# Copies that form the weight sums wait for a tile of the gated projection or of the attention

## The chip, the cores and the metric

The kernel runs on one core of a Trainium2 chip. The core has TensorE (PE) for matmuls, with its weight loads shown apart (PEld), VectorE (DVE), ScalarE (ACT), GpSimd (POOL) and SyncE (SP). DMAs are commands in the queue of the engine that issues them, here nearly all SP or POOL; the bytes are moved by 16 DMA engines that all queues share. The metric is the device time of the program in microseconds (us): 1652.23 as the median of three runs, 1650.91 to 1655.87.

## The reference

One layer of a decoder on 1024 tokens of width 1024, in float32. From a normalised input one projection makes queries, six key and value blocks, gates, a pooling input and merge-gate logits:

```
h = rms_norm(x, norm_mix);  proj = h @ w_in
a = nsa_attention(q, kv, gates, ...) @ w_branch_attn    # compressed, selected and window branch
b = pool_mixer(u_pool, pool_w, pool_scale) @ w_branch_pool
ga, gb = split(sigmoid(g_merge), 2)
x = x + (ga * a + gb * b) @ w_out
h = rms_norm(x, norm_mlp)
x = x + square(relu(h @ w_ff1)) @ w_ff2;  return rms_norm(x, norm_final)
```

There are 8 heads of 64 in two groups, blocks of 64 keys, a window of 512, and an MLP of width 4096.

## The kernel before

Every float32 operand is split into a high part, which ScalarE rounds to the matmul's format (hi, L179), and a low part, the rest, which POOL or VectorE subtracts (lo, L82). A product is three matmuls: high by high (L77), high by low (L78, L79). Weights come through one helper, `load`: a raw tile of 128x512 (`wraw`, 4 buffers, a DMA on SP, L178), then `whi` and `wlo` (3 buffers each).

The stages, in the order of the program:

1. First key/value block (L230 to 268), to 53 us: x and weights are loaded and multiplied into eight PSUM banks.
2. Second key/value block and compression (L283 to 381): `block2` in eight token tiles, `compress` for keys and values; `keys` rotates and transposes keys.
3. Query blocks (`qblock`, L383 to 400), twice eight token tiles: 24 matmuls of 256 columns, `q` made by ScalarE (L392, two buffers), rotated by POOL (L145 to 149), stored to DRAM as `qd` (L395).
4. Pooling mixer (`pool_in`, `pool_mix`, four groups): 48 matmuls of 512 columns for each group, then 6 more. The low parts of the weights are made by POOL.
5. Gated projection (L480 to 501): eight blocks m of 48 matmuls for the gate and 24 for the branch, each giving two tiles `gb` (two buffers, stored to DRAM as `gbd`). Low parts by POOL, three per block.
6. Attention: 32 pairs (query tile i, head pair hp), scores and softmax of one pair woven with transposes and values of the pair before. Between them `ga_terms` is fed in, a gate projection of eight weight blocks, two low parts each, by POOL. A finished pair writes its part of `oT` (L666).
7. Merge: the attention's output projection, `ta` and `gb` loaded back (L796, L797, `gb` with one buffer), then `w_out`.
8. The MLP. It uses seven block products in place of eight, for which sums of weight blocks are needed.

These sums are the change's subject. Each of 32 is a tile of 1 MB in DRAM: a plain copy of one block from DRAM to DRAM on SP's queue (L208), then a DMA on POOL's queue that adds a second block, or an earlier sum, to it (L213, L216). The function `weight_sums` is a generator: one step issues one copy and the accumulation of the step before.

```
206                         d = dram.tile([P, 2048], F32, name=f"ws{layer}{fh}{p}{h}")
208                         nc.sync.dma_start(d, a[layer][fh, m0, k0, h])
213                             nc.gpsimd.dma_start(d_, src, accum_op=ADD, max_dma_last_dim=2048)
```

The program calls `next(sums)` once in each block m of the gated projection (L481) and then from `advance` (L689) as the attention goes on. That doesn't set when a copy runs. The framework orders each engine's instructions when the program is built, by its own estimate of when each could start, and waits are semaphores that it places for tiles read and written. The copies read an input and write a fresh tile, so nothing holds them back, and in the order that it finds they stand on SP from the second key/value block on, between the loads and stores of that stage, with the accumulations on POOL.

Of the kernel before, what the change touches and what calls it, by code (L numbers as in the profile page):

```python
# [17 lines left out]
P = 128  # L18
S = 1024
# [30 lines left out]
def build(tc, a, out, dbg=None):  # L50
    nc = tc.nc
# [141 lines left out]
    tad = [[dram.tile([P, HALF], F32, name=f"tad{m}_{h}") for h in range(2)] for m in range(NK)]  # L193


    wsum = {}

    def weight_sums():
        late = []
        for layer in ("w_ff1", "w_ff2"):  # L200
            for fh in range(2):
                for p in (7, 6, 5, 3):
                    for h in range(2):
                        d = dram.tile([P, 2048], F32, name=f"ws{layer}{fh}{p}{h}")
                        wsum[layer, fh, p, h] = d
                        (m0, k0), (m1, k1) = {7: ((0, 0), (1, 0)), 6: ((1, 1), (0, 0)), 5: ((1, 0), (1, 1)),
                                              3: ((0, 1), (0, 0))}[p]
                        nc.sync.dma_start(d, a[layer][fh, m0, k0, h])  # L208
                        prior = {6: 7, 3: 6}.get(p)
                        late.append((d, a[layer][fh, m1, k1, h] if prior is None else wsum[layer, fh, prior, h]))  # L210
                        if len(late) > 1:
                            d_, src = late.pop(0)
                            nc.gpsimd.dma_start(d_, src, accum_op=ADD, max_dma_last_dim=2048)  # L213
                        yield
        for d_, src in late:
            nc.gpsimd.dma_start(d_, src, accum_op=ADD, max_dma_last_dim=2048)  # L216

    sums = weight_sums()


# [201 lines left out]
    with ExitStack() as st:  # L422
# [6 lines left out]
        with ExitStack() as st2:  # L429
# [48 lines left out]
                    pool_mix(*prev)  # L478
                prev = cur
            for m in range(NK):  # L480
                next(sums)  # L481
                gh, gl = load(cols(a["w_in"], C_GB + m * P, P))
                bh, bl = load(cols(a["w_branch_pool"], m * P, P, 0, 4))
                zz = []
                for hf in range(2):
                    sl = slice(hf * HALF, (hf + 1) * HALF)
                    ps = psF.tile([P, HALF], F32, name="psF")
                    mm3(ps, [(gh[:, k], gl[:, k], XH[k][:, sl], XL[k][:, sl]) for k in range(NK)])
                    z = wg.tile([P, HALF], F32, name="z", bufs=3)
                    nc.vector.tensor_tensor(z, ps, rB[:, sl], op=MUL)  # L490
                    nc.scalar.activation(z, z, AF.Tanh, scale=0.5)
                    zz.append(z)
                if m == 0:
                    pool_mix(*prev)
                for hf in range(2):
                    sl = slice(hf * HALF, (hf + 1) * HALF)
                    ps = psF.tile([P, HALF], F32, name="psF")
                    mm3(ps, [(bh[:, k], bl[:, k], mxh[:, k, sl], mxl[:, k, sl]) for k in range(4)])
                    gb = wg.tile([P, HALF], F32, name="gb", bufs=2)
                    nc.vector.scalar_tensor_tensor(gb, zz[hf], 1.0, ps, op0=ADD, op1=MUL)  # L500
                    nc.sync.dma_start(gbd[m][hf], gb)


    octx = ExitStack()
# [2 lines left out]
    with ExitStack() as st:  # L507
# [175 lines left out]
        done, given, summed = 0.0, 0, 0  # L683

        def advance(w):
            nonlocal done, given, summed
            done += w
            while summed < 26 * done / total:
                next(sums, None)  # L689
                summed += 1  # L690
            while given < nterm and given < nterm * done / total:
                next(fill, None)
                given += 1
# [5 lines left out]
        for n in range(len(pairs) + 1):  # L699
            aseq = []  # L700
            if n < len(pairs):
                i, hp = pairs[n]
                if n == 12:
                    sctx.close()
                    psS = pool(sctx, "psS2", bufs=2, space=PSUM)
                u, aseq = units_a(i, hp, q)
                if hp % 2:
                    def nxt(j=2 * i + hp // 2 + 1):
                        nonlocal q, qnext
                        if j < 2 * NT:  # L710
                            q = split_q(qnext)
                            if j + 1 < 2 * NT:
                                qnext = load_q((j + 1) // 2, (j + 1) % 2)
                    aseq.append(nxt)
            na, nslot = len(aseq), max(1, sum(o for _, o in bseq))
            ia = k = 0
            for fn, slot in bseq or [(None, True)]:
                if fn is not None:
                    fn()
                if slot:  # L720
                    k += 1
                    while ia < na and ia * nslot < k * na:
                        aseq[ia]()
                        ia += 1
                    advance(bw / nslot)
            assert ia == na
            if n < len(pairs):
                bseq, bw = units_b(u), weight[n]
        for _ in fill:
            pass  # L730
        for _ in sums:
            pass
        sctx.close()
        dump("oT", oT)
    psTctx.close()
# [289 lines left out]
```

## Time and profile before

| | |
|---|---|
| median of three runs | 1652.23 us (1650.91 to 1655.87) |
| profiled execution: time, span | 1656.69 us, 1654.9 us |
| granted TensorE clock, mean | 0.943 |
| busy share of the span | PE 89%, PEld 74%, DVE 61%, ACT 46%, POOL 10% |
| DMA queues, share of 16 engines' span | q1 (SP) 32.8%, q0 (POOL) 11.5% |
| HBM read, written | 186.52 MB, 83.89 MB |
| copies of the weight sums on SP | 32 issued, 33.3 to 319.1 us |
| accumulations on POOL | 32 issued, 41.4 to 341.4 us |

The span runs from the first to the last instruction. The stages stand in it so: first key/value block to 53 us, second block with compression to about 150, query blocks to 265, pooling mixer to 356, gated projection to 490, attention to 850, merge to about 1000, MLP to the end. A granted clock of 1.00 is 2.4 GHz, 0.50 is 1.2. A DMA share is the mean busy share of 16 engines and can come out above 1 where packets overlap. "Landing" is the time from a DMA's issue to its last byte.

### The profile page before, as it was taken

How to read it: one execution, taken by the hardware profiler on the slowest of the kernel's cores; microseconds unless marked ns; L12 is line 12 of the kernel's file. 1: busy time of each engine (PE TensorE's matmuls, PEld its weight loads, DVE VectorE, ACT ScalarE, POOL GpSimd, SP SyncE). 2: the span in 40 equal slices, each digit the busy share in tenths (PEclk: the TensorE clock that was granted, in tenths of full speed). 3: DMA queues.
4: the chain of work that ended last, by engine and by line, in shares of the span. 5: the costliest groups of instructions: out<-in, count | busy, mean ns of one | idle time of the engine just before them, and what ended most of it. 6: DMA issues, size and time to landing. Idle time of an engine off the chain costs nothing.

```text
span 1654.9 us, 20716 instructions
## 1 busy us (share of the span) xinstructions
PE 1480.2 (89%) x7369; PEld 1222.5 (74%) x7369; DVE 1001.7 (61%) x1928; ACT 758.6 (46%) x1561; POOL 169.1 (10%) x206
## 2 busy tenths in 40 slices
PE   8766554669999999999998989999999999999995
PEld 6755453558877788887876878888888888888874
DVE  5554101331118888887765575766789656669984
ACT  4332110121227877777753344557434453764441
POOL 2111333122220000000001010000000000001020
PEclk9878677789999999999999999999999999999997
DMA  8999999962231110010046533333333333333322
GB/s 304 289 286 222 262 275 280 230 144 83 77 102 46 38 46 21 33 33 26 27 136 214 148 104 107 94 100 97 97 95 97 96 96 96 96 96 97 96 63 102
DMA packets 130137, 204.67 MB, mean 124 GB/s; under 512 B 9840, under 2 KB 62832, under 8 KB 129520
## 3 DMA queue, kind: packets, MB, share of 16 engines
q1 hardware_dynamic: 112992, 169.78, 32.8%
q0 software_dynamic: 16896, 33.56, 11.5%
q8 instruction: 58, 0.95, 0.2%
q14 instruction: 47, 0.39, 0.1%
q10 hardware_dynamic: 144, 0.00, 0.0%
HBM read 186.52 MB, written 83.89 MB: 163 GB/s over the span
## 4 chain that ended last, share of the span: by engine, by line
PE 71%; DMA 3%; DVE 3%; ACT 2%; issue 1%; POOL 0%; POOLq 0%; DVEq 0%; SPq 0%; ACTq 0%
PE psm L79 14%; PE psm L77 14%; PE psm L78 14%; PE oacc L659 5%; PE psT L648 4%; PE psF L79 3%; PE psF L78 3%; PE psF L77 3%; DMA gb<-gbd 3%; PE psS L553 2%; PE psS L554 2%; PE psG L77 2%; PE psG L78 2%; PE psG L79 2%; PE psS L556 1%
## 5 line engine op out<-in xcount | busy, mean ns | idle before, releaser
L78 PE MATMUL psm<-mv,whi 128*128 128x512 f32 x896 | 351.9, 393 | 0.0
L77 PE MATMUL psm<-mv,whi 128*128 128x512 f32 x896 | 351.8, 393 | 0.0
L79 PE MATMUL psm<-mv,wlo 128*128 128x512 f32 x896 | 351.7, 393 | 0.0
L82 DVE TENSOR_TENSOR wlo<-wraw,whi 128x512 fp32r<-128x512 f32 x288 | 197.9, 691 | 109.9 <-ACT whi L858 70.3
L858 ACT CAST whi<-wraw 128x512 fp32r<-128x512 f32 x224 | 138.8, 620 | 247.9 <-PE psm L78 185.9
L78 PEld LDWEIGHTS psm<-mv,whi 128*128 128x128 f32 x896 | 169.0, 189 | 37.0
L77 PEld LDWEIGHTS psm<-mv,whi 128*128 128x128 f32 x896 | 168.9, 189 | 36.9
L79 PEld LDWEIGHTS psm<-mv,wlo 128*128 128x128 f32 x896 | 168.9, 188 | 36.8
L179 ACT CAST whi<-wraw 128x512 fp32r<-128x512 f32 x112 | 69.4, 622 | 175.3 <-PE psF L78 77.0
L79 PE MATMUL psF<-xh,wlo 128*128 128x512 f32 x192 | 79.1, 412 | 50.7 <-POOL wlo L82 50.7
L652 DVE TENSOR_TENSOR pl<-psT,ph 128x512 fp32r<-128x512 f32 (+1 forms) x160 | 101.9, 646 | 31.1 <-ACT ph L651 29.7
L754 POOL TENSOR_TENSOR sqa<-sqa,sq 128x512 f32<-128x512 f32 x24 | 33.1, 1381 | 803.0 <-ACT sq L750 803.0
L651 ACT CAST ph<-psT 128x512 fp32r<-128x512 f32 (+1 forms) x160 | 87.6, 555 | 50.1 <-PE psT L648 48.4
L563 DVE TENSOR_REDUCE nm<-psS 128x1 f32<-128x64 f32 (+8 forms) x192 | 99.6, 539 | 16.4 <-PE psS L556 9.0
L82 POOL TENSOR_TENSOR wlo<-wraw,whi 128x512 fp32r<-128x512 f32 x48 | 64.3, 1350 | 422.5 <-ACT whi L179 299.3
L77 PE MATMUL psF<-bhi,xh 128*128 128x256 f32 (+1 forms) x192 | 63.9, 335 | 40.0 <-ACT q L392 15.1
L79 PEld LDWEIGHTS psF<-xh,wlo 128*128 128x128 f32 x192 | 38.3, 199 | 60.2 <-POOL wlo L82 52.0
L77 PE MATMUL psF<-xh,whi 128*128 128x512 f32 x192 | 78.4, 408 | 2.8 <-ACT q L392 2.8
L78 PE MATMUL psF<-xl,whi 128*128 128x512 f32 x192 | 78.0, 406 | 0.0
L77 PEld LDWEIGHTS psF<-bhi,xh 128*128 128x128 f32 x192 | 43.9, 230 | 42.8 <-ACT q L392 15.4
L564 ACT ACTIVATE pS<-psS,nm 128x64 f32<-128x64 f32 (+8 forms) x128 | 67.9, 532 | 8.3 <-DVE nm L563 7.9
L838 ACT CAST mv<-mt 128x512 fp32r<-128x512 f32 x96 | 59.1, 617 | 20.0 <-DVE mt L836 15.5
(241 smaller groups left out, 3119.1 us busy)
## 6 DMA issues: line engine op xcount, KB each, us to landing
wraw<-wsw_ff SPq DMA_DIRECT2D x128, 256.0 KB, 3.1
wraw<-in_w_ff SPq DMA_DIRECT2D x96, 256.0 KB, 3.1
wsw_ff<-in_w_ff POOLq DMA_DIRECT2D x16, 1024.0 KB, 27.2
wsw_ff<-wsw_ff POOLq DMA_DIRECT2D x16, 1024.0 KB, 18.0
wraw<-in_w_in SPq DMA_DIRECT2D x40, 256.0 KB, 2.9
wraw<-in_w_out SPq DMA_DIRECT2D x32, 256.0 KB, 3.1
xt<-in_x SPq DMA_DIRECT2D x8, 512.0 KB, 5.2
qd<-q SPq DMA_DIRECT2D x16, 256.0 KB, 8.7
```

Source lines behind the costliest of these rows:

```text
L77: nc.tensor.matmul(ps, lhsT=sh, rhs=mh, start=first and i == 0, stop=False, skip_group_check=more)
L78: nc.tensor.matmul(ps, lhsT=sh, rhs=ml, start=False, stop=False, skip_group_check=more)
L79: nc.tensor.matmul(ps, lhsT=sl, rhs=mh, start=False, stop=last and i == n - 1, skip_group_check=more)
L82: eng.tensor_tensor(lo, src, f(hi), op=SUB)
L179: nc.scalar.copy(h, v)
L563: nc.vector.tensor_reduce(nm, v, axis=AX.X if flat else AX.XY, op=MAX, negate=True)
L564: nc.scalar.activation(p if flat else p.rearrange("p (a n) -> p a n", a=2), v, AF.Exp, bias=nm, accum_out=sm)
L648: nc.tensor.transpose(ps[:, j, e], src[e][:, c0:c0 + P], ident)
L651: nc.scalar.copy(ph[:, :n], ps[:, :n])
L652: nc.vector.tensor_tensor(pl[:, :n], ps[:, :n], f(ph[:, :n]), op=SUB)
L659: nc.tensor.matmul(o, lhsT=v, rhs=part[:rows, j], start=gi == 0 and j == 0 and part is ph, stop=2 * gi + j == nb - 1 and part is pl)
L858: nc.scalar.copy(hi, raw)
```

## The change

A copy of a weight sum now goes to POOL's queue. Ahead of it, on SP, four words (16 bytes) of a tile just computed are stored into the sum's own tile. The copy writes over them, so it must wait for that store, and the store for the tile. The tiles are kept in a list `made`: in the gated projection the last `gb` of the block before (L505 after the change; the first block has none, so seven sums start there), in the attention the part of `oT` of the pair before last, one sum at most per pair, 25 in all, the last of them behind the last part of `oT`.

```diff
--- before.py
+++ after.py
@@ -193,7 +193,8 @@
     tad = [[dram.tile([P, HALF], F32, name=f"tad{m}_{h}") for h in range(2)] for m in range(NK)]
 
 
-    wsum = {}
+
+    wsum, made = {}, []
 
     def weight_sums():
         late = []
@@ -205,7 +206,8 @@
                         wsum[layer, fh, p, h] = d
                         (m0, k0), (m1, k1) = {7: ((0, 0), (1, 0)), 6: ((1, 1), (0, 0)), 5: ((1, 0), (1, 1)),
                                               3: ((0, 1), (0, 0))}[p]
-                        nc.sync.dma_start(d, a[layer][fh, m0, k0, h])
+                        nc.sync.dma_start(d[0:1, 0:4], made.pop())
+                        nc.gpsimd.dma_start(d, a[layer][fh, m0, k0, h])
                         prior = {6: 7, 3: 6}.get(p)
                         late.append((d, a[layer][fh, m1, k1, h] if prior is None else wsum[layer, fh, prior, h]))
                         if len(late) > 1:
@@ -478,7 +480,8 @@
                     pool_mix(*prev)
                 prev = cur
             for m in range(NK):
-                next(sums)
+                if made:
+                    next(sums)
                 gh, gl = load(cols(a["w_in"], C_GB + m * P, P))
                 bh, bl = load(cols(a["w_branch_pool"], m * P, P, 0, 4))
                 zz = []
@@ -499,6 +502,7 @@
                     gb = wg.tile([P, HALF], F32, name="gb", bufs=2)
                     nc.vector.scalar_tensor_tensor(gb, zz[hf], 1.0, ps, op0=ADD, op1=MUL)
                     nc.sync.dma_start(gbd[m][hf], gb)
+                made[:] = [gb[0:1, 0:4]]
 
 
     octx = ExitStack()
@@ -683,11 +687,8 @@
         done, given, summed = 0.0, 0, 0
 
         def advance(w):
-            nonlocal done, given, summed
+            nonlocal done, given
             done += w
-            while summed < 26 * done / total:
-                next(sums, None)
-                summed += 1
             while given < nterm and given < nterm * done / total:
                 next(fill, None)
                 given += 1
@@ -724,12 +725,19 @@
                         ia += 1
                     advance(bw / nslot)
             assert ia == na
+            if n >= 2 and summed < 25 * done / total:
+                i, hp = pairs[n - 2]
+                made[:] = [oT[0:1, hp, i * P:i * P + 4]]
+                next(sums, None)
+                summed += 1
             if n < len(pairs):
                 bseq, bw = units_b(u), weight[n]
         for _ in fill:
             pass
-        for _ in sums:
-            pass
+        while len(wsum) < 32:
+            made[:] = [oT[0:1, 3, S - 4:S]]
+            next(sums)
+        next(sums, None)
         sctx.close()
         dump("oT", oT)
     psTctx.close()
```

What it moves on the engines is seen in their order. On SP in the second query block and at the start of the pooling mixer, before the change (`qd` are stores of queries, `wsw_ff` the sums, `s` the mixer's weights):

```order
L208 DMA wsw_ff_5786<-in_w_ff 16x16384
L395 DMA qd_104<-q 128x512
L395 DMA qd_105<-q 128x512
L208 DMA wsw_ff_5961<-in_w_ff 16x16384
L208 DMA wsw_ff_6122<-in_w_ff 16x16384
L395 DMA qd_106<-q 128x512
L395 DMA qd_107<-q 128x512
L208 DMA wsw_ff_6270<-in_w_ff 16x16384
L208 DMA wsw_ff_6437<-in_w_ff 16x16384
L395 DMA qd_108<-q 128x512
L395 DMA qd_109<-q 128x512
L208 DMA wsw_ff_6610<-in_w_ff 16x16384
```

The same place after it:

```order
L397 DMA qd_102<-q 128x512
L178 DMA wraw<-in_w_in 128x4x128 x2
L397 DMA qd_103<-q 128x512
L397 DMA qd_104<-q 128x512
L397 DMA qd_105<-q 128x512
L397 DMA qd_106<-q 128x512
L397 DMA qd_107<-q 128x512
L397 DMA qd_108<-q 128x512
L397 DMA qd_109<-q 128x512
L435 DMA s<-in_pool_w 128x4x128
L178 DMA wraw<-in_w_in 128x4x128 x3
```

Six copies stood among these stores and loads; none does now. On POOL in the pooling mixer before the change (`pwl` and `wlo` are low parts, `u` a tile's margin):

```order
L213 DMA wsw_ff_6610<-in_w_ff 512x512
L82 TENSOR_TENSOR pwl<-s,pwh 128x512
L82 TENSOR_TENSOR wlo<-wraw,whi 128x512 x2
L213 DMA wsw_ff_6766<-wsw_ff_6437 512x512
L213 DMA wsw_ff_6918<-wsw_ff_6610 512x512
L439 MEMSET u 128x16
L82 TENSOR_TENSOR wlo<-wraw,whi 128x512
L213 DMA wsw_ff_7089<-in_w_ff 512x512
L82 TENSOR_TENSOR wlo<-wraw,whi 128x512
L213 DMA wsw_ff_7235<-in_w_ff 512x512
L213 DMA wsw_ff_7387<-wsw_ff_6766 512x512
L439 MEMSET u 128x16
```

After it, to the first sum in the gated projection:

```order
L82 TENSOR_TENSOR pwl<-s,pwh 128x512
L82 TENSOR_TENSOR wlo<-wraw,whi 128x512 x2
L441 MEMSET u 128x16
L82 TENSOR_TENSOR wlo<-wraw,whi 128x512 x2
L441 MEMSET u 128x16
L82 TENSOR_TENSOR wlo<-wraw,whi 128x512 x7
L210 DMA wsw_ff_2524<-in_w_ff 16x16384
L82 TENSOR_TENSOR wlo<-wraw,whi 128x512
L215 DMA wsw_ff_2524<-in_w_ff 512x512
L82 TENSOR_TENSOR wlo<-wraw,whi 128x512 x2
L210 DMA wsw_ff_2633<-in_w_ff 16x16384
```

The accumulations that stood between the mixer's low parts are gone, and the first copy stands behind all of the mixer's low parts and those of the first two blocks of the gated projection. On POOL at the passage from the gated projection to the attention after the change, where before there was only a run of 41 low parts:

```order
L82 TENSOR_TENSOR wlo<-wraw,whi 128x512 x2
L210 DMA wsw_ff_3183<-in_w_ff 16x16384
L82 TENSOR_TENSOR wlo<-wraw,whi 128x512
L215 DMA wsw_ff_3183<-wsw_ff_2743 512x512
L82 TENSOR_TENSOR wlo<-wraw,whi 128x512 x2
L210 DMA wsw_ff_3553<-in_w_ff 16x16384
L215 DMA wsw_ff_3553<-wsw_ff_2853 512x512
L210 DMA wsw_ff_3722<-in_w_ff 16x16384
L82 TENSOR_TENSOR wlo<-wraw,whi 128x512
L215 DMA wsw_ff_3722<-in_w_ff 512x512
L82 TENSOR_TENSOR wlo<-wraw,whi 128x512
L210 DMA wsw_ff_4026<-in_w_ff 16x16384
```

In a block of the gated projection a copy stands ahead of the next block's first low part and the accumulation behind it; in the attention one or two low parts, or none, stand between a copy and the next. On SP at the end of the attention after the change (`tad` stores the gates, `ta` and `gb` are the merge's first loads):

```order
L538 DMA tad_1_139<-z 128x512
L178 DMA wraw<-in_w_branch_attn 128x4x128
L209 DMA wsw_ff_7821<-oT 1x4
L538 DMA tad_0_140<-z 128x512
L209 DMA wsw_ff_7942<-oT 1x4
L178 DMA wraw<-in_w_branch_attn 128x4x128 x2
L538 DMA tad_1_141<-z 128x512
L209 DMA wsw_ff_7946<-oT 1x4
L804 DMA ta<-tad_0_126 128x512
L805 DMA gb<-gbd_0_110 128x512
```

The last two small stores stand close ahead of the merge's first loads, and the last one waits for the end of the attention. On PE, DVE and ACT the same instructions stand before and after; in the second key/value block, the compression and the query blocks some stand a few places earlier or later, and from the gated projection on none does.

## Rows read from the trace of the kernel before

**Rows 1.** Busy time by stretches: stretch, us, busy by engine, clock, DMA share, GB/s
```profile
53.00:150.00 97.00, 63.04 (x389) 58.08 (x387) 54.24 (x163) 34.03 (x87) 10.85 (x13) 0.81 1.07 288
150.00:265.00 115.00, 70.19 (x415) 64.68 (x414) 14.52 (x67) 20.59 (x46) 42.92 (x97) 0.77 1.04 256
265.00:356.00 91.00, 42.18 (x150) 33.44 (x151) 28.02 (x32) 11.41 (x17) 21.23 (x22) 0.70 1.02 233
356.00:490.00 134.00, 132.80 (x584) 109.11 (x583) 28.75 (x41) 27.87 (x44) 30.68 (x25) 1.00 0.27 77
490.00:850.00 360.00, 351.89 (x2286) 286.25 (x2284) 287.48 (x676) 269.83 (x686) 17.51 (x14) 1.00 0.12 36
```

**Rows 2.** DMA view, 60 to 340 us: queues; issues with median landing
```profile
q0 software_dynamic: 15354, 30.50, 61.8%
q1 hardware_dynamic: 14150, 43.13, 43.6%
...
wsw_ff<-in_w_ff POOLq DMA_DIRECT2D x14, 1024.0 KB, 29.2
qd<-q SPq DMA_DIRECT2D x16, 256.0 KB, 8.7
...
wsw_ff<-in_w_ff SPq DMA_DIRECT2D x28, 14.2
```

**Rows 3.** The same of 380 to 480 us, in the gated projection
```profile
q1 hardware_dynamic: 11232, 7.87, 27.1%
...
gbd<-gb SPq DMA_DIRECT2D x12, 256.0 KB, 2.0
```

**Rows 4.** Waits, 53 to 150 us: who waited for whom, total, times, longest
```profile
ACT bhi L179 <- DMA wraw<-in_w_in: 13.5, 7, 5.2
PEld psH L77 <- ACT whi L179: 13.0, 3, 9.6
ACT whi L179 <- DMA wraw<-in_cmp_k_w: 12.8, 2, 11.2
...
ACT whi L179 <- DMA wraw<-in_cmp_v_w: 10.9, 6, 3.5
```

**Rows 5.** Waits, 150 to 265 us
```profile
ACT q L392 <- DMA qd<-q: 66.8, 13, 15.7
```

**Rows 6.** Waits, 265 to 357 us
```profile
PE psF L79 <- POOL wlo L82: 50.7, 3, 23.8
POOL wsw_ff L213 <- DMA wsw_ff<-in_w_ff: 46.0, 6, 12.3
```

**Rows 7.** TensorE in order of time: start, us, instruction, idle before
```profile
80.04 0.28 PE L79 MATMUL psH<-whi,Xl 128*128 128x256 f32 x1
80.16 0.28 PE L77 MATMUL psH<-whi,Xh 128*128 128x256 f32 x1
...
94.29 0.58 PE L77 MATMUL psH<-whi,Xh 128*128 128x256 f32 x1 [9.40 <-ACT whi L179]
...
97.22 0.42 PE L79 MATMUL psH<-whi,Xl 128*128 128x256 f32 x1
97.43 0.42 PE L77 MATMUL psH<-whi,Xh 128*128 128x256 f32 x1
```

**Rows 8.** POOL in order of time, one block of the gated projection
```profile
383.27 1.29 POOL L82 TENSOR_TENSOR wlo<-wraw,whi 128x512 fp32r<-128x512 f32 x1 [6.87 <-ACT whi L179]
386.00 1.29 POOL L82 TENSOR_TENSOR wlo<-wraw,whi 128x512 fp32r<-128x512 f32 x1 [1.43 <-ACT whi L179]
391.43 1.29 POOL L82 TENSOR_TENSOR wlo<-wraw,whi 128x512 fp32r<-128x512 f32 x1 [4.14 <-ACT whi L179]
399.59 1.29 POOL L82 TENSOR_TENSOR wlo<-wraw,whi 128x512 fp32r<-128x512 f32 x1 [6.87 <-ACT whi L179]
```

**Rows 9.** Groups of POOL, 265 to 357 us: count, busy, mean ns, idle before
```profile
L213 POOL DMA_DIRECT2D wsw_ff<-wsw_ff x4 | 4.1, 1015 | 36.1 <-DMA wsw_ff<-in_w_ff 36.1
```

**Rows 10.** Chain of waits after the attention, in order of time
```profile
858.21 6.26 DMA gb<-gbd
```

## The prediction

> **What bounds the kernel now.** I read the busy time by stretches first, since the page's shares are means over stages with different limits. From 356 us on TensorE is the bound: busy 132.8 of 134 us in the gated projection and 351.9 of 360 in the attention, at a granted clock of 1.00, with the DMA engines at 0.27 and 0.12 [rows 1]. Ahead of that it is not. From 53 to 356 us, in the second key/value block with the compression, in the query blocks and in the pooling mixer, TensorE is busy 63.0 of 97, 70.2 of 115 and 42.2 of 91 us, at clocks of 0.81, 0.77 and 0.70, while the DMA share stands at 1.02 to 1.07, and no other engine comes near its limit except VectorE with 54.2 of the first 97 us [rows 1]. So the first third waits for DMA, and the next question is whose bytes those are.
>
> The DMA view of 60 to 340 us answers it. Queue q0 holds only the accumulating halves of the weight sums, and they keep all 16 engines for 61.8% of these 280 us, 173 us for 29 of them, 6.0 us each [rows 2]. Queue q1 took 122 us (43.6%) for 43.1 MB: 28 plain copies of 1.05 MB, 29.4 MB, and 13.8 MB of the stage's own traffic. In the gated projection, where q1 carries nothing but own traffic, 7.87 MB took 27.1 us, 3.44 us per MB [rows 3]; so the 13.8 MB account for 47 us and the copies for 75 us, 2.7 us each. One weight sum is thus 8.7 us of all DMA engines, and the 32 are 278 us, four times what the stages there need for themselves. Their harm is seen in landings: a store of queries takes 8.7 us [rows 2] where the like store gbd of the gated projection takes 2.0 [rows 3].
>
> Then the waits, stretch by stretch. 53 to 150: ScalarE, which makes the high part of each weight, waits 13.5, 12.8 and 10.9 us for three streams of weights to land [rows 4]. 150 to 265: ScalarE waits 66.8 us for stores of q, since q has two buffers [rows 5]. 265 to 356: TensorE waits 50.7 us, in three pieces of up to 23.8, for low parts that POOL makes, and POOL stands 46.0 us in front of accumulations whose copies have not landed [rows 6].
>
> **The change part by part.** It takes 32 copies out of SP's queue and gives them to POOL, each behind a 16-byte store on SP that waits for a tile: seven for gb of the gated projection, 25 for oT of the attention. The work of PE, DVE and ACT is the same instruction for instruction; in the block stages some of it stands a few places earlier or later. SP gains 32 small stores and loses 32 copies, so its number of commands stays; POOL gains 32 commands. Before 356 us no copy and no accumulation is left.
>
> *53 to 150 us, now 97.* The three waits of ScalarE add up to 37.2 us; without them 60 would remain. VectorE's 54.2 us of work is a floor under that [rows 1, 4]. First loads still have a latency, so I take 65. Bounds: 54, and 84 if only the 13.0 us go that TensorE itself stood for these weights [rows 4].
>
> *150 to 265 us, now 115.* 16 query tiles go through two buffers; a landing of 2.0 us in place of 8.7 takes 16 x 6.7 / 2 = 54 us off and leaves 61. From TensorE's side: 384 matmuls of 256 columns, which follow each other every 0.12 us at the higher of its two clock levels, 2.4 GHz (80.04 to 80.16) [rows 7], are 46 us, and about 3 for transposes, an estimate. I take 55, the middle of 49 and 61. The upper bound is 88: at the lower level, 1.2 GHz, which TensorE had after standing still for 9.4 us, the same matmul takes 0.21 us (97.22 to 97.43) [rows 7], 384 of them 82 us, and 6 for the passages between blocks (an estimate).
>
> *265 to 356 us, now 91.* 192 matmuls of the projection and 18 of the mixer. The gated projection repeats every 16.32 us (383.27 to 399.59) for 72 such matmuls [rows 8], 0.227 us each, so 210 take 47.7. I take 51, with 3 for the start. The waits that go (50.7) are more than the slack that is there, so TensorE's own work is the floor; the upper bound is 60, half of the longest wait staying. Sum of the three: 303 us become 171, **132 us less** (bounds 70 and 152).
>
> *Gated projection.* Here the new waits stand in POOL's queue among the low parts that TensorE needs. A low part made at 383.27 is followed by one at 386.00 and one at 391.43 [rows 8]. The block before which the first is made began 8.9 us earlier (36 matmuls, then ACT), at 374.4. The copy waits for the previous block's last gb, some 0.8 us into the block, then for a store with 2.0 us of landing [rows 3]: it starts at about 378, ahead of 383.27, and delays nothing. The accumulation stands between the first and the second low part and waits for the copy. The second is ready at 387.3 and needed at 374.4 + 16.3 + 2.7 = 393.4, a slack of 6.1 us; the copy may thus land up to 14 us after its start. No row shows a copy on POOL's queue. Between the 2.7 us of engine time worked out above and the 14.2 us median that copies on SP took among saturated engines [rows 2], I take 5 (2.7 and a store's landing of 2.0), nearer the lower, since the share here comes to 0.27 + 7 x 8.7 / 134 = 0.72. Cost: 0; at 14.2 it is 0.2 us in each of seven blocks, 1.4. Weights are loaded a block ahead, so slower loads are hidden too.
>
> *Attention.* 25 sums in 360 us, one per 14.4; DMA share 0.12 + 25 x 8.7 / 360 = 0.72. POOL needs 5 us of waiting and two issues of 1.0 [rows 9] per sum, 7 in all, and keeps up. With a landing of 14.2 it needs 16.2, falls behind by 1.8 us at each of the 21 sums ahead of its last low part, 38 us, against the 22 us by which a low part is early (half of the 45 us that eight weight blocks have each in 360): 16 us of cost. A gain is excluded, since TensorE is busy for 351.9 us of this stage. I take 4, for the query loads at its start, which share the engines with the end of the seventh sum; bounds 0 and 16.
>
> *After the attention.* The last two sums can begin only with the last oT; 17.4 us of DMA time fall into the merge, whose chain is a row of loads of gb, one after another, of up to 6.3 us [rows 10]. Half of the 17.4, 8 us, is my value; bounds 0 and 17.
>
> Sum: -132 + 4 + 8 = **-120 us**. The profiled run took 1656.7 us with a span of 1654.9, so it becomes 1537; the median of the three timed runs is 1652.2, 4.5 lower, hence **1532 us**.
>
> **The rivals.**
> *Beginning held by other things.* The engines' order is fixed ahead, and at low clock TensorE needs 0.21 us per small matmul. With the first stretch at its upper bound and the others halfway to theirs (84, 75, 54), 303 become 213, 90 less; with +12 given back the time is 1574. For it: the clocks of 0.70 to 0.81. Against: at 70 to 140 us there are pieces at full clock, and 356 to 490 runs at 1.00 once weights arrive.
> *Given back.* The sums meet the stages they were moved to at their upper bounds, 1 + 16 + 17, and as much again on the first loads of each stage, 68 in all: -132 + 68 gives 1588. For it: a DMA share of 0.72 where loads stood alone. Against: most loads there are issued a block ahead.
> *At the floor.* All three stretches at their lower bounds, nothing given back: 1652 - 152 = 1500.
> *POOL becomes the pace.* If a copy on POOL's queue lands as late as the accumulations did, 29.2 us [rows 2], then each of seven gated blocks waits 15 us (106), and POOL needs 31 us per sum, 16.8 more than 14.4, for 21 sums (350), less the 22 of slack: 106 + 328 - 132, slower by some 300, about 1950. It decides from a landing of about 19 us (7 x 5 + 21 x 6.6 - 22 = 152, the whole gain at its best). Against: the rows with 29.2 come from engines at over 1.0. The Trainium skill (SBUF — State Buffer, SBUF: two separate sides) gives this rival a second way: descriptors of a DMA issued by POOL are written by POOL itself, and some VectorE instructions lock it out meanwhile. VectorE is busy for 287.5 of the attention's 360 us [rows 1], and no row shows POOL issuing beside that; by the rule the copies of the attention alone would start late.
> *The sums don't spread*, and all bunch elsewhere; the order of SP and POOL speaks against it. About 1652.
>
> **How the numbers follow.** Forecast 0.53, beginning held 0.15, given back 0.13, floor 0.12, POOL the pace 0.05, no spread 0.02. The range of 1498 to 1582 holds the forecast (alone 1510 to 1555), the floor and the held beginning. Runs of this kernel lie within 0.3% of each other, so less than that can't be told from no change: faster 0.93, same 0.02, slower 0.05.
>
> **What would show it.** Right: from 53 us to the start of the gated projection (first z) about 170 us in place of 303, DMA share there under 0.4, clock above 0.9; stores of q landing in 2 to 3 us; no wait of TensorE for POOL in the pooling mixer; copies on q0 landing in about 5 us, one per 14 us in the attention, which stays at 360 to 365; the merge up to 8 us longer. Wrong: TensorE waiting for POOL's low parts in the gated projection or the attention; the block stages staying above 230 us with the DMA engines idle, which would mean that the copies had only stood beside another limit.

## The result, and the profile after

The kernel after the change takes **1520.16 us** (median of 4 runs, 1519.52 to 1521.38), beside 1652.59 us for the kernel before on the same chip (4 runs, 1650.91 to 1655.87). The ratio is 0.920 (95% interval 0.918 to 0.921): 132 us less, 12 us below the forecast of 1532. The profiled execution took 1521.4 us with a span of 1519.6; before, the span was 1654.9, so the traces differ by 135.3 us.

Busy time of the kernel after by stretches, with the columns of [rows 1]. The windows are the same stages as there, which now begin earlier: second block with compression, query blocks, pooling mixer, gated projection, attention.

```profile
53.00:112.00 59.00, 52.93 (x386) 49.28 (x385) 50.08 (x153) 31.06 (x81) 1.09 (x3) 0.97 0.24 70
112.00:160.00 48.00, 44.78 (x364) 43.34 (x364) 14.69 (x68) 20.13 (x45) 29.07 (x80) 1.00 0.44 138
160.00:207.00 47.00, 46.82 (x206) 38.36 (x205) 29.84 (x34) 12.37 (x18) 14.64 (x17) 1.00 0.19 51
207.00:340.00 133.00, 132.23 (x581) 108.59 (x579) 28.19 (x41) 27.61 (x44) 41.06 (x38) 1.00 0.72 179
340.00:708.00 368.00, 356.25 (x2288) 290.48 (x2288) 289.06 (x679) 270.99 (x689) 55.34 (x62) 0.98 0.71 173
```

In the first three rows TensorE (first number after the length) is now busy for all but 6.1, 3.2 and 0.2 us of the stage, the clock stands at 0.97 to 1.00 where [rows 1] has 0.70 to 0.81, and the DMA share fell from over 1 to 0.19 to 0.44. In the last two rows it rose from 0.27 and 0.12 to 0.72 and 0.71. TensorE stays the bound there, but in the attention its clock is 0.98 where it was 1.00 [rows 1].

Marks split the 135 us: the first and the last `q`, the first `z` of the gated projection, the first and the last `ot` (the result of a pair) of the attention. Their rows, each with the first and the last start, first of the kernel before, then of the kernel after:

```profile
L392 ACT ACTIVATE q<-psF,req x16: 687/687/689, 152.3 to 261.0; 128x512 f32<-128x512 f32 x16
L490 DVE TENSOR_TENSOR z<-psF,rB x16: 683/691/692, 362.4 to 483.4; 128x512 f32<-128x512 f32 x16
L663 ACT COPY ot<-oacc x32: 367/367/370, 502.5 to 850.8; 64x256 f32<-64x256 f32 x32
```

```profile
L394 ACT ACTIVATE q<-psF,req x16: 680/688/690, 112.6 to 158.7; 128x512 f32<-128x512 f32 x16
L493 DVE TENSOR_TENSOR z<-psF,rB x16: 683/692/692, 213.2 to 334.2; 128x512 f32<-128x512 f32 x16
L667 ACT COPY ot<-oacc x32: 367/368/371, 359.5 to 707.5; 64x256 f32<-64x256 f32 x32
```

| us | before | after | difference |
|---|---|---|---|
| 53 us to first `q` | 99.3 | 59.6 | -39.7 |
| first to last `q` | 108.7 | 46.1 | -62.6 |
| last `q` to first `z` | 101.4 | 54.5 | -46.9 |
| first `z` to first `ot` | 140.1 | 146.3 | +6.2 |
| first to last `ot` | 348.3 | 348.0 | -0.3 |
| last `ot` to the end | 804.1 | 812.1 | +8.0 |

The first third gives 149.2 us, and 14 come back at two places.

The waits of ScalarE for the stores of q, 66.8 us in [rows 5], have become these two rows (112 to 160 us of the kernel after: who waited for whom, total, times, longest):

```profile
ACT q L394 <- PE psF L79: 8.6, 8, 2.4
ACT q L394 <- DMA qd<-q: 5.6, 3, 2.8
```

ScalarE now waits more for TensorE's products than for the stores. Of the waits in [rows 6], that of TensorE for POOL's low parts is gone from the mixer, where TensorE stands for 0.2 us in all.

The sums, where they went. The DMA view of the kernel after, 345 to 700 us in the attention (queues: packets, MB, share of 16 engines; then issues, with KB each and median us to landing where the trace has them):

```profile
q0 software_dynamic: 12893, 49.09, 59.7%
q1 hardware_dynamic: 12734, 12.55, 11.5%
...
wsw_ff<-in_w_ff POOLq DMA_DIRECT2D x12, 1024.0 KB, 8.9
wsw_ff<-wsw_ff POOLq DMA_DIRECT2D x11, 1024.0 KB, 9.6
...
wsw_ff<-in_w_ff POOLq DMA_DIRECT2D x24, 5.2
```

An accumulation of an input block lands in 8.9 us, in place of 29.2 [rows 2], one of an earlier sum in 9.6, in place of 18.6; a copy on POOL's queue lands in 5.2. POOL in order of time, around one sum of the gated projection:

```profile
246.38 0.55 POOL L210 DMA_DIRECT2D wsw_ff<-in_w_ff  x1 [2.85 <-DMA wsw_ff<-gb]
250.40 1.28 POOL L82 TENSOR_TENSOR wlo<-wraw,whi 128x512 fp32r<-128x512 f32 x1 [3.47 <-ACT whi L179]
251.94 1.03 POOL L215 DMA_DIRECT2D wsw_ff<-in_w_ff  x1 [0.26 <-DMA wsw_ff<-in_w_ff]
253.12 1.29 POOL L82 TENSOR_TENSOR wlo<-wraw,whi 128x512 fp32r<-128x512 f32 x1
258.56 1.29 POOL L82 TENSOR_TENSOR wlo<-wraw,whi 128x512 fp32r<-128x512 f32 x1 [4.15 <-ACT whi L179]
```

The brackets tell how long POOL stood and for what: 0.26 us for the copy, 2.85 for the small store, the rest for ScalarE's high parts. The low parts follow each other at 250.40, 253.12 and 258.56, the distances of [rows 8]. That holds for the first two sums. In the last five blocks POOL stands 1.7 to 2.6 us for the copy, and the second low part starts 3.7 to 4.6 us behind the first in place of 2.7; the blocks still follow each other every 16.32 us, so TensorE loses nothing by it. In the attention POOL stands much longer for the sums (365 to 706 us, who waited for whom), but no wait of another engine names POOL:

```profile
POOL wsw_ff L210 <- DMA wsw_ff<-oT: 123.6, 18, 9.6
POOL wsw_ff L215 <- DMA wsw_ff<-in_w_ff: 74.1, 14, 10.2
```

The first place where time comes back is the start of the attention (340 to 365 us, waits):

```profile
DVE ql L553 <- ACT qh L552: 8.9, 2, 8.5
ACT qh L552 <- PE psT L549: 8.2, 1, 8.2
...
PE psT L549 <- DMA qi<-qd: 4.6, 1, 4.6
```

Read from below: a load of queries (`qi`) is late, TensorE waits 4.6 us for it, and ScalarE and VectorE behind it. The accumulation of the seventh sum was issued just ahead of these loads:

```profile
335.93 1.03 POOL L215 DMA_DIRECT2D wsw_ff<-wsw_ff  x1 [2.64 <-DMA wsw_ff<-in_w_ff]
```

The second place is the merge, in the chain of waits:

```profile
709.66 6.67 DMA gb<-gbd
717.69 7.90 DMA gb<-gbd
726.41 7.97 DMA gb<-gbd
```

The first loads, which took 2.7 to 6.3 us before (the longest is in [rows 10]), take 6.7 to 8.0. Beside them the last two sums still run on POOL's queue:

```profile
704.18 1.03 POOL L215 DMA_DIRECT2D wsw_ff<-wsw_ff  x1 [5.15 <-DMA wsw_ff<-in_w_ff]
714.35 0.52 POOL L210 DMA_DIRECT2D wsw_ff<-in_w_ff  x1 [9.13 <-DMA wsw_ff<-oT]
721.55 1.02 POOL L218 DMA_DIRECT2D wsw_ff<-wsw_ff  x1 [6.68 <-DMA wsw_ff<-in_w_ff]
```

### The profile page after: what moved, and what is told of

Same layout as the page of the kernel before. It is cut to its first block, busy times and chain, and to the rows that moved or that the text cites. A ratio compares the mean times of both kernels' runs of the same rounds, so it can differ in the third digit from the quotient of the medians.

```text
span 1519.6 us, 20787 instructions
## 1 busy us (share of the span) xinstructions
PE 1454.1 (96%) x7369; PEld 1200.8 (79%) x7369; DVE 1002.5 (66%) x1928; ACT 760.2 (50%) x1561; POOL 186.9 (12%) x238
## 4 chain that ended last, share of the span: by engine, by line
PE 84%; DVE 6%; DMA 6%; ACT 2%; issue 1%; POOL 1%; SPq 0%; POOLq 0%; DVEq 0%; ACTq 0%
PE psm L79 15%; PE psm L77 15%; PE psm L78 15%; PE oacc L663 5%; PE psF L78 5%; PE psF L79 5%; PE psF L77 5%; PE psT L652 4%; DMA gb<-gbd 3%; PE psS L557 3%; PE psS L558 2%; PE psG L77 2%; PE psG L78 2%; PE psG L79 2%; PE psS L560 1%
## 5 line engine op out<-in xcount | busy, mean ns | idle before, releaser
L77 PE MATMUL psm<-mv,whi 128*128 128x512 f32 x896 | 351.2, 392 | 0.0
L77 PE MATMUL psF<-xh,whi 128*128 128x512 f32 x192 | 74.7, 389 | 0.0
L79 PE MATMUL psF<-xh,wlo 128*128 128x512 f32 x192 | 74.7, 389 | 0.0
L78 PE MATMUL psF<-xl,whi 128*128 128x512 f32 x192 | 74.7, 389 | 0.0
L82 DVE TENSOR_TENSOR mv<-mt,mv 128x512 fp32r<-128x512 f32 x96 | 67.3, 707 | 1.1 <-ACT mv L846 0.6
L663 PE MATMUL oacc<-ph,vst 128*128 128x256 f32 x264 | 64.3, 318 | 1.2 <-ACT ph L655 0.9
L652 PE MATMUL psT<-cf,pS 128*128 128x128 f32 x352 | 60.5, 276 | 2.1 <-DVE pS L624 2.0
```

The costliest lines, as they stand in the source:

```text
L77: nc.tensor.matmul(ps, lhsT=sh, rhs=mh, start=first and i == 0, stop=False, skip_group_check=more)
L78: nc.tensor.matmul(ps, lhsT=sh, rhs=ml, start=False, stop=False, skip_group_check=more)
L79: nc.tensor.matmul(ps, lhsT=sl, rhs=mh, start=False, stop=last and i == n - 1, skip_group_check=more)
L82: eng.tensor_tensor(lo, src, f(hi), op=SUB)
L652: nc.tensor.transpose(ps[:, j, e], src[e][:, c0:c0 + P], ident)
L663: nc.tensor.matmul(o, lhsT=v, rhs=part[:rows, j], start=gi == 0 and j == 0 and part is ph, stop=2 * gi + j == nb - 1 and part is pl)
```

## The experiments

The first four kernels ask why the first third was so slow. Theory **A**: one sum costs so much time of the 16 DMA engines, whichever queue its commands stand in and whenever POOL issues them, that the sums alone filled the engines. Rival **B**: the copies stood ahead of loads and stores in SP's queue. Rival **C**: POOL stood before the accumulations, and TensorE's low parts behind it. The next four price what still comes back, the last four repeat two kernels, look for a better pace and split the cost of a sum. Each group ran on a chip of its own, and ratios are against the kernel before on that chip (medians 1655.47, 1659.25 and 1657.42 us).

**Only the queue changed, no waiting.** From the kernel before:

```
-                        nc.sync.dma_start(d, a[layer][fh, m0, k0, h])
+                        nc.gpsimd.dma_start(d, a[layer][fh, m0, k0, h])
```

> The kernel before with one line changed: the copies go to POOL's queue, without the small store and its wait. The wait alone is undone, the queue is that of the change. Theory A (the first third waits for the 16 DMA engines' time, whichever queue fills them): the 278 us of copies and accumulations still lie ahead of the gated projection, so the time stays near 1652 us, between 1620 and 1690, first z at 340 us or later, DMA share near 1 to there. Theory B (loads and stores stood behind copies in SP's own queue): freed of that, the first third loses most of what the change took off, 1560 us or less. Theory C (POOL standing before the sums is what delays TensorE): POOL now stands in front of 32 more commands, so slower than 1652 by 20 us or more.

1636.79 us, ratio 0.989 (0.986 to 0.992). Its DMA view of 60 to 340 us:

```profile
q0 software_dynamic: 14575, 54.55, 79.7%
q1 hardware_dynamic: 15902, 15.44, 19.3%
...
qd<-q SPq DMA_DIRECT2D x16, 256.0 KB, 7.9
...
wsw_ff<-in_w_ff POOLq DMA_DIRECT2D x27, 13.4
```

SP's queue is free of copies, but the engines are as full (79.7 and 19.3%), and a store of q still takes 7.9 us in place of 8.7 [rows 2]. So B does not explain the loss. The 19 us are no clean price of the queue: the copies now start at 1.3 us in place of 33.3, TensorE is busy for 33.8 of the first 53 us in place of 47.0, and a copy and three accumulations are issued only behind the first `z`, where before none was left.

**Only the waiting, the queue as before.** From the kernel after:

```
-                        nc.gpsimd.dma_start(d, a[layer][fh, m0, k0, h])
+                        nc.sync.dma_start(d, a[layer][fh, m0, k0, h])
```

> The changed kernel with the copies back on SP's queue, each still behind the small store of gb or oT. The queue alone is undone. Theory A: the same DMA work at the same places, so 1520 us within 8, first z at 213 us. Theory B: SP now stands for each small store to land, 2 us, with the loads of weights and queries behind it, and the loads stand behind copies; the gated projection and the attention lose some us for each of 32 sums, 1545 us or more.

1527.68 us (2 runs, 1522.69 and 1532.66), ratio 0.924 (0.916 to 0.932); the first `z` at 213.4 us, after the change 213.2. The moment of the sums decides, not their queue. Whether POOL's queue is worth anything against SP's stays inside the interval.

**Early copies, no accumulations.** From the kernel before:

```
-                        if len(late) > 1:
-                            d_, src = late.pop(0)
-                            nc.gpsimd.dma_start(d_, src, accum_op=ADD, max_dma_last_dim=2048)
...
-        for d_, src in late:
-            nc.gpsimd.dma_start(d_, src, accum_op=ADD, max_dma_last_dim=2048)
```

> The kernel before without its accumulations: the MLP reads sums that hold only their first block (the second block's addition is left out), all else stays, the 32 copies on SP among the loads. Theory A: of 278 us of DMA time 86 remain ahead of the gated projection, no more than the stages can hide, so most of the gain shows, 1510 to 1550 us, first z before 245 us, and the landing of the stores of q falls to 3 to 5 us. Theory B: the copies still stand ahead of loads in SP's queue, so 1600 us or more, stores of q still above 7. Theory C: POOL stands before nothing, the 50 us of the pooling mixer go, about 1600.

1518.3 us, ratio 0.919 (0.913 to 0.924). All copies stand early on SP, and yet the first third is nearly that of the kernel after: busy time from 53 us to the first `z`, and two rows of the DMA view of 60 to 230 us:

```profile
53.00:221.00 168.00, 152.46 (x977) 137.28 (x978) 100.91 (x262) 65.54 (x146) 44.82 (x99) 0.98 0.79 264
```

```profile
q1 hardware_dynamic: 16763, 43.12, 75.5%
...
qd<-q SPq DMA_DIRECT2D x16, 256.0 KB, 2.9
```

With the engines at 0.79, a store of q lands in 2.9 us and TensorE's clock is at 0.98. The copies alone cost the first third 8 us (168 in place of 160); the accumulations carry the loss.

**Low parts of the mixer's weights on VectorE.** From the kernel before:

```
-                wh, wl = load(cols(a["w_in"], C_POOL + m * P, P))
+                wh, wl = load(cols(a["w_in"], C_POOL + m * P, P), nc.vector)
```

> The kernel before with one edit: the pooling mixer's low parts are made by VectorE in place of POOL, so that no low part of that stage stands behind an accumulation on POOL. Theory A: the weights themselves land late and ScalarE waits for them in place of POOL, 0 to 20 us off, 1632 to 1652 us. Theory C: the 50.7 us of waits for POOL go, 1600 to 1612 us.

1640.58 us, ratio 0.994 (0.988 to 1.001). TensorE's 50.7 us of waits for POOL in the mixer [rows 6] are down to one of 8.1, and others stand in their place (240 to 345 us):

```profile
DVE wlo L82 <- ACT whi L179: 26.1, 2, 21.3
...
PE psF L77 <- ACT plh L460: 24.9, 2, 21.6
ACT pwh L434 <- DMA s<-in_pool_w: 21.6, 1, 21.6
...
PEld psF L79 <- POOL wlo L82: 8.6, 1, 8.6
```

TensorE's longest wait is 21.6 us for ScalarE, which has itself stood 21.6 us for the mixer's weights to land. It stood 21.5 for them in the kernel before too, where the wait of 23.8 then read as one for POOL: for this wait C was the last link of a chain that begins at the DMA engines. C may have a small share of its own: the first `z` comes 17.6 us earlier, though 0.988 to 1.001 includes no gain.

**No sums at all.** From the kernel after:

```
-                        d = dram.tile([P, 2048], F32, name=f"ws{layer}{fh}{p}{h}")
-                        wsum[layer, fh, p, h] = d
...
-                        nc.sync.dma_start(d[0:1, 0:4], made.pop())
-                        nc.gpsimd.dma_start(d, a[layer][fh, m0, k0, h])
...
+                        wsum[layer, fh, p, h] = a[layer][fh, m0, k0, h]
```

> The kernel after the change with no weight sums at all: small stores, copies and accumulations are left out, and the MLP reads one input block in place of each sum, so its numbers are not the layer's. If what the spread sums still cost is what the two traces show, 6 us at the first pair of the attention and 9 in the merge, the time falls by 15 from 1520 to about 1505, and the first third stays at 160 us from 53 us to the first z. If the sums also slow the stages between in ways that the waits do not show (weight loads, clock), it falls by clearly more, to under 1495. If the 9 us of the merge belong to something else, such as its loads being issued at once, it falls only to about 1514.

1505.99 us, ratio 0.908 (0.905 to 0.911). The first `z` stands at 213.5 us, from there to the first `ot` it takes 140.2 us, the pairs 346.5, the rest 803.7. So in the kernel after the sums cost nothing before the first `z`, 6.1 at the attention's start and 8.4 behind it. The 1.5 us in its course are not theirs: the kernels with no sums in the attention take 346.5 to 348.9 for it. That is 14.5 us by the traces; the ratios, 0.920 and 0.908 on two chips, give 19.

**Six sums in the gated projection, 26 in the attention.** From the kernel after:

```
-                if made:
+                if made and m < NK - 1:
...
-            if n >= 2 and summed < 25 * done / total:
+            if n >= 2 and summed < 26 * done / total:
```

> The seventh sum of the gated projection, whose accumulation was issued at 336 us just ahead of the attention's first loads, is put into the attention: six sums in the gated projection, 26 in the attention. If the 6 us lost at the first pair come from that accumulation holding the engines while the first query loads wait, they go, and the time is about 1514. Rival: another sum falls on the same place or the loads are late anyway; then it stays at 1520.

1516.9 us, ratio 0.914 (0.912 to 0.917), 3 us more than expected. From the first `z` to the first `ot` it takes 142.4 us in place of 146.3, two thirds of the loss. TensorE's wait for `qi` is 0.25 us in place of 4.6, but its granted clock is 0.77 in the 15 us from 341, where it is 1.00 without sums; these are the other 2 us, and what lowered it there I did not find. It is not simply the six sums: of the three profiles below with the same six ahead and a closer pace in the attention, two show 1.00 there and one 0.89.

**The attention's sums closer.** From the kernel after:

```
+        NS = 25
...
-            if n >= 2 and summed < 25 * done / total:
+            if n >= 2 and summed < min(NS, NS * done / (0.8 * total)):
```

> The 25 sums of the attention follow each other faster, one per 0.8 of their former distance, so that the last starts behind pair 28 of 32 and none is left for the merge. If the merge's 9 us come from the DMA time of the last sums beside its loads of gb, they go: about 1511. If POOL then falls behind with the low parts (a copy of 5.2 us and an accumulation per 11 us in place of 14), TensorE waits in the attention and the time stays at 1520 or rises. If the merge's loss is not from the sums, 1520.

1516.47 us, ratio 0.914 (0.911 to 0.916), 5 us more than expected. Behind the last `ot` it takes 803.6 us, as without sums: the merge's loss was the last sums' DMA time. But the attention takes 352.8 us from first to last `ot` in place of 348.0, and 4 us of that stand at one place. VectorE and POOL of this kernel in order of time there:

```profile
475.42 0.19 DVE L618 RECIPROCAL cc<-cc 128x6 f32<-128x6 f32 x1
475.64 2.31 DVE L619 TENSOR_TENSOR cc<-cc,sg 128x6 f32<-128x6 f32 x1
477.99 0.48 DVE L624 TENSOR_SCALAR pS<-pS,cc 128x512 f32<-128x512 f32 x1
```

```profile
475.08 1.03 POOL L215 DMA_DIRECT2D wsw_ff<-wsw_ff  x1 [9.15 <-DMA wsw_ff<-in_w_ff]
475.74 0.89 POOL L210 DMA_DIRECT2D wsw_ff<-in_w_ff  x1
476.27 1.65 POOL L82 TENSOR_TENSOR wlo<-wraw,whi 128x512 fp32r<-128x512 f32 x1
```

A product of 128x6 words, which takes 0.17 us elsewhere, takes 2.31 while POOL issues an accumulation, the next copy and makes a low part without a break; it ends at 477.95, the low part at 477.92. TensorE waits 1.86 us for what follows, and its clock is 0.88 from 470 to 484 us, where it is 1.00 without sums. The pace, not the amount, costs here: in the kernel after, where no such burst held VectorE for more than 1.3 us, the attention lost nothing against before.

**Both edits**, with 26 sums at 0.75 of their distance:

> Both edits: six sums in the gated projection, 26 in the attention at 0.75 of their former distance. If both places are priced rightly and independent, 6 + 9 go: about 1505, the same as without any sums. If the faster pace costs the attention what the merge gains, 1512 to 1520.

1509.61 us, ratio 0.910 (0.907 to 0.912). That is 5 us more than the 1505 for two independent gains, and 2 us below the range of the other case. The start of the attention is free (140.1 us from `z` to `ot`), the part behind the last `ot` takes 804.1, but the attention takes 351.2. Two such places are in the trace: at 556.73 and 569.26 us VectorE instructions of 0.25 to 0.61 us take 2.5 to 2.8, and at the second the attention falls 3.2 us behind the kernel without sums.

**Again, beside the kernel after.** No edit against the two kernels named:

> The kernel after the change once more, so that the variants of this call stand beside it on one chip: 1520.

> Six sums in the gated projection and 26 at 0.75 of their distance in the attention, again, beside the kernel after the change: 1510, thus 0.993 of it.

1522.17 us (ratio 0.919, 0.916 to 0.922) for the kernel after, 1511.66 (0.911, 0.908 to 0.914) for the closer pace. As expected, within 2 us. The loss at the attention's start is not a constant: in this profile of the kernel after it takes 149.2 us from `z` to `ot`, in the first 146.3, with a wait for `qi` of 6.9 us in place of 4.6.

**The same with a pace of 0.85.** From the kernel of both edits:

```
-            if n >= 2 and summed < min(NS, NS * done / (0.75 * total)):
+            if n >= 2 and summed < min(NS, NS * done / (0.85 * total)):
```

> As the variant with six sums in the gated projection and 26 in the attention, but at 0.85 of their former distance in place of 0.75. There, twice, a copy was issued right behind an accumulation with a low part of POOL behind it, and instructions of VectorE that otherwise take 0.2 to 0.6 us took 2.5 to 2.8; the attention lost 3.3 us at the second such place. If the closer pace causes this, no such instruction is seen here, the attention is 347 us long from first to last ot in place of 351, and unless the last sum now runs into the merge the time is 1506, about that without any sums. If the last accumulation runs into the merge's first loads, that takes it back: 1510 to 1514.

**1507.64 us**, ratio 0.910 (0.907 to 0.912), the lowest median of a version with all sums, 14.5 us below the kernel after on the same chip (the interval overlaps that of the pace of 0.75). From `z` to `ot` 140.1 us, the attention 348.3, the rest 803.8. No VectorE instruction of the attention is held for more than 1.5 us. The last accumulation is issued at 697.59 us, 3.5 ahead of the last `ot`, and the loads of `gb` behind it take 2.8 to 6.2. By these marks nothing of what the sums cost is left beyond the scatter of the attention's length; by the ratios, 0.910 and 0.908 with intervals that overlap, at most a few us.

**Plain copies in place of additions.** From the kernel before, at both places:

```
-                            nc.gpsimd.dma_start(d_, src, accum_op=ADD, max_dma_last_dim=2048)
+                            nc.gpsimd.dma_start(d_, src, max_dma_last_dim=2048)
```

> The kernel before with its order unchanged, but the second DMA of each sum a plain copy of the same shape in place of an addition, so that the sums are wrong. It tells what in the accumulations fills the engines: if it is the addition, the second DMAs take about 2.7 us of all engines in place of 6.0, the DMA share of the first third falls below 0.9 and the time goes most of the way to the 1518 of the kernel without accumulations, to 1530 to 1560. If it is their form (512 rows of 2 KB on POOL's queue), they still take about 6.0 us and the time stays at 1640 to 1660.

1605.17 us, ratio 0.968 (0.965 to 0.971). Neither end came. Its DMA view of 60 to 300 us:

```profile
q1 hardware_dynamic: 15480, 43.19, 52.3%
q0 software_dynamic: 8187, 31.54, 40.6%
...
qd<-q SPq DMA_DIRECT2D x16, 256.0 KB, 9.2
```

A second DMA without the addition takes 3.2 us of all engines (0.406 x 240 us over the 30 that the 31.54 MB make) in place of 6.0 [rows 2], so the addition makes nearly half of an accumulation's price. It doesn't come alone: without it the packets are 3.9 KB in the mean (31.54 MB in 8187), with it 2.0 (30.50 in 15354), and the run doesn't part the two. But the engines stay full (0.92 to the first `z`), so the stage only ends sooner. My expectation of 1530 to 1560 took the copies' price off a stage that was still bound by them.

All kernels of the question in one table, from 53 us to the first `z`. The engine time is share by length.

| kernel | length, us | DMA share | engine time, us | clock |
|---|---|---|---|---|
| before | 309.4 | 1.03 | 319 | 0.77 |
| mixer's low parts on VectorE | 291.8 | 1.07 | 312 | 0.78 |
| copies early on POOL's queue | 281.6 | 0.99 | 279 | 0.84 |
| plain copies in place of additions | 252.9 | 0.92 | 233 | 0.82 |
| early copies, no accumulations | 168.0 | 0.79 | 133 | 0.98 |
| waiting copies on SP | 160.4 | 0.29 | 47 | 0.99 |
| after | 160.2 | 0.28 | 45 | 0.99 |
| no sums | 160.5 | 0.29 | 47 | 0.98 |

While the engine time is above 160 us, the length follows it; below, the length stays at 160 to 168, of which TensorE is busy for 151. That is theory A, with a floor. Where the share is near 1 the two agree by construction; what tests the theory is that prices read in one kernel carry to another: 46 us of own traffic and 29 copies at 2.7 make 124 for the early copies, where 133 are measured. The first three rows differ in how much of the sums runs ahead of 53 us and behind the first `z`, so their lengths are not to be compared closely. The rate in bytes would not have told: 233 to 288 GB/s in [rows 1], and 264 with no accumulations and half the length.

## Why the prediction was right, and where it was off

- **What bounds the kernel.** That the first third waited for DMA time, and that this time was the sums', held: the table above, and the run without accumulations, show it. The waits for loads, for stores and for low parts were three faces of one cause.
- **The first third, -132, measured -149.** This is the term that was mis-sized, by 17 us, and the miss comes from it: 15 us between the traces, of which 12 show in the medians, since the profiled run lay 4.5 us above its median before and 1.2 after. The three stretches gave 39.7, 62.6 and 46.9 us where 32, 60 and 40 were forecast and 43, 66 and 43 were the bounds. I had added a margin to each floor, for first loads, for the landings of the stores and for starting up; little of it is there, since TensorE is busy now for all but 6.1 of 59, 3.2 of 48 and 0.2 of 47 us. The last stretch even beat its bound, since its mark is the first `z` and not the stage's edge. The rival of the floor was right for this term. Two figures on the way were off without weight: the sums' 278 us are six times the stages' own 47, not four, and 384 matmuls at 0.21 us are 81 us, not 82.
- **Gated projection, 0, measured 0.** The seven copies land in 5.2 us, where 5 was taken, and the second low part came up to 1.9 us late, within the 6.1 us of slack.
- **Attention, +4, measured +5.9.** Its place was named rightly, the first query loads beside the seventh sum (4.6 us of waiting). Behind the first pair the difference to before stays within 1 us.
- **After the attention, +8, measured +8.0.** The place and the cause are right, since with the sums ended earlier the loss goes. The size is luck: half of two whole sums was a guess, and the accumulation of the last but one was issued 3.3 us ahead of the last `ot`, so only one sum began behind it.
- **Beginning held by other things** (1574): fell. The clock rose as soon as the weights arrived; in the table it is 0.77 to 0.84 with 233 us of engine time or more and 0.98 to 0.99 with less, with the same instructions on TensorE.
- **Given back** (1588): the terms were their middle values, not their ends.
- **POOL becomes the pace** (1950): POOL does wait, 124 us and 74 us in the attention, but its low parts are early enough. The second way, VectorE keeping POOL from issuing, was not seen: with VectorE busy for 289 of 368 us, a copy's issue takes 0.51 to 0.91 us and the copy lands in 5.2. The reverse was seen: POOL's burst held VectorE for 2.3 to 2.8 us. The Trainium skill (SBUF — State Buffer, Who interferes with whom) has both directions in one rule: GpSimd and some kinds of VectorE instruction share a pair of ports, and whichever issues first holds it for its whole instruction. The traces agree as far as the short instructions that are held end with POOL's low part, within 0.1 us, and those that take 0.61 us elsewhere 0.4 to 0.5 behind it; which of POOL's three instructions took the ports, no run here tells.
- **No spread** (1652): fell.

## What to carry to other kernels

Background traffic that has no reader for a long time should be tied to a tile of a stage with idle DMA engines, since an order that only looks at when something could start puts it where it fills them; multiply the DMA share by the stretch's length, and where this engine time exceeded TensorE's own work in the stretch, the DMA engines were the bound here, whatever the waits named. Of the ways to spread it, the moment counts and the queue hardly does; leave a gap ahead of the next stage's first loads and end before the last. Where TensorE's own work is at hand as a floor and nothing else is queued there, forecast the floor, not a margin above it.

## What the hardware showed that I had not expected

- A DMA that adds takes 6.0 us of all 16 engines for 1 MB, the same command without the addition 3.2, and a plain copy on SP's queue 2.7 (an estimate, as in the prediction, from what the stage's own traffic leaves). The packets are of 2.0 and 3.9 KB in the first two, and all three ran among engines over 0.9 busy.
- A POOL sequence of accumulation, copy and low part can hold a VectorE instruction of 0.17 us for 2.31, and a low part by itself held one of 0.25 us for 1.28 (in the kernel without sums too, at 420 us). In the kernel with sums at 0.75 of their distance, two of the eight low parts that took 1.60 to 1.68 us, as in such a sequence, came with a hold over 2.3 us.
